# Row additions of the first expert round split between GpSimd and VectorE and tied behind the last gate product; a second convolution by transposes; a router shift summed before its product

## The chip, the cores and the metric

The kernel runs on one core of a Trainium2 chip. Its time is the device time in microseconds (us) of one execution; several runs are made and their median is taken. Lower is better. The engines are named as in the profile: PE (TensorE, matrix products and transposes), DVE (VectorE), ACT (ScalarE), POOL (GpSimd) and SP (SyncE, which here only issues transfers). Each engine works through its own instructions in order.

## The reference

Two layers of a diffusion backbone over 256 latent rows of width 1024, with 256 context rows that go through layer 0 whole and through layer 1 only as keys and values. What matters here is the end of a layer:

```python
    x = x + g1 * _merge(attn, hyena, gates, w_br_a, w_br_b, w_out)
    h2 = _rms(x, norm_ffn) * (1.0 + sc2) + sh2
    x = x + g2 * _hier_moe(h2.reshape(B * L, D), w_group, b_group, w_router, b_router,
                           moe_w1, moe_w3, moe_w2).reshape(B, L, D)
...
    for g in range(N_GROUPS):
        a = jnp.einsum('td,edf->tef', h, w1[g])
        b = jnp.einsum('td,edf->tef', h, w3[g])
        hid = jax.nn.silu(a) * b * cw[:, g, :, None]
        y = y + jnp.einsum('tef,efd->td', hid, w2[g], preferred_element_type=F32)
```

Of the 32 experts of a layer each row uses two. The context rows do the same with `g2c` in place of `g2`. Inside the merge, `hyena` is a long convolution of order two, `z = gate * (conv + z * skip)` once for each order.

## The kernel before

Rows are held in tiles of 128: in layer 0 four of them (`i` = 0 and 1 latent, 2 and 3 context), in layer 1 two. A framework places the instructions of each engine in an order that it fixes when the program is built.

**The first expert round** (`first_round`) takes the 32 experts in 16 pairs p; `q` counts 0 to 7 and each `q` holds the pairs 2q and 2q+1. For a pair, PE makes the product `w13` (tile `pW<-we,xT`, 32 recorded matmuls of 128x512), ACT the silu (`sl`), DVE the gate product `hd` (L1365), PE transposes it (`pX<-cst,hd`, L1368), ACT copies it (`hdT`), and PE makes `w2` (`pW<-we,hdT`, 16 recorded matmuls). I write hd(p), w13(p) and w2(p) for those of pair p. The weights come as loads of 1 MiB, six for a pair, from SP's queue into a ring of buffers; `fetch` issues a load when the buffer's last user has been put in the program.

The results of `q` < 6 are scattered by POOL to rows of a DRAM buffer `ybuf`. Those of `q` = 6 and 7 stay on the chip as `Y` and reach the rows by products with a selection matrix (`pG<-Y,PT`, `pQ<-Y,PT`, L1456). What was scattered is read back by `collect(i)`: two loads of 128x1024 from POOL's queue (`yr`, `yt`), and an inner function `add` with three VectorE operations of 128x1024: sum of the two, times the gate row `g2` (a broadcast, tile `bc`), added to `x`. `collect` of the first half of the tiles is called at `q` = 6, that of the rest at `q` = 7; the `add`s of each follow the next gate product in the code. After the pairs comes a branch for rows that found no place (`overflow`), which these inputs do not need.

**Layer 1's start** (`head`): the rows are normalised (`xn`, L457), transposed by PE, scaled, split in two parts (`hT`), and multiplied with the input weights in pieces; the first pieces give `u`, on which DVE does two operations a piece (L535, L537) for a short convolution before PE transposes it. The context rows' last additions (`rest`) stand in this stretch on DVE.

**The second convolution's output** is made in three places (layer 0 twice, layer 1 once) by 48 matmuls of 128x128 (`pB<-gt,Yh`), each followed on DVE by the product with `x2`. **The router's shift** (L890) is, in the same three cases, a product of a matrix of ones with eight slices of 128x36 (16 records).

## Time and profile before

| | before |
|---|---|
| median of 3 runs | 1447.03 us (1446.01 to 1447.13) |
| profiled execution, time | 1441.07 us |
| profiled execution, span | 1439.3 us |
| mean granted TensorE clock | 0.961 |
| PE busy | 1281.0 us, 89% |
| VectorE busy | 660.3 us, 46% |
| ScalarE busy | 455.8 us, 32% |
| GpSimd busy | 211.0 us, 15% |
| DMA, mean | 259 GB/s |

The profiled execution is one of its own, beside the three timed runs; the span goes from its first to its last instruction. PE is busy nearly everywhere, so the places to look at are the few where it stands still.

### The profile page before, as it was taken

To read this page: it belongs to the slowest core of one execution; us is meant where nothing else is said; L and a number is where in the kernel's file an instruction comes from. 1 tells how busy PE (TensorE), PEld (TensorE's weight loads), DVE (VectorE), ACT (ScalarE), POOL (GpSimd) and SP (SyncE) were. 2 spreads that over 40 slices of the span, in tenths; PEclk is the share of its full clock that TensorE was granted. 3 is DMA by queue.
4 is the path that set the end of the run, shared out by engine and by line. 5 is a ranking of instruction groups with operands and counts; after the bars stand their busy time and mean duration, and the time that the engine had idled before them with its cause. 6 is when DMAs were issued, how large, how long until landed. Compare 5 with 4: busy or idle time off the path is not lost. (4 is left out here: it accounts for less than half of the span.)

```text
span 1439.3 us, 18183 instructions
## 1 busy us (share of the span) xinstructions
PE 1281.0 (89%) x7071; PEld 831.1 (58%) x7071; DVE 660.3 (46%) x1361; ACT 455.8 (32%) x884; POOL 211.0 (15%) x175
## 2 busy tenths in 40 slices
PE   5999999999999999599888397999899969998776
PEld 2555777886578887344333134899779943443222
DVE  4654366676677666601000137865774760100014
ACT  3433223337632133222211014533574522221101
POOL 2021033361000000211110000032500021110000
PEclk9999999999999999699999699999999979999989
DMA  9744625455177762799999963325326749999991
GB/s 377 282 166 185 230 90 190 159 219 215 59 262 274 288 241 98 278 408 420 419 420 422 403 274 137 129 106 211 136 94 219 259 161 380 418 419 420 422 407 69
DMA packets 65691, 373.04 MB, mean 259 GB/s; under 512 B 11994, under 2 KB 13338, under 8 KB 26048
## 3 DMA queue, kind: packets, MB, share of 16 engines
q1 hardware_dynamic: 54368, 347.67, 61.9%
q0 software_dynamic: 10368, 21.02, 4.1%
q10 hardware_dynamic: 864, 3.15, 0.5%
q8 instruction: 57, 0.93, 0.3%
q14 instruction: 34, 0.28, 0.1%
HBM read 362.06 MB, written 27.53 MB: 271 GB/s over the span
## 5 line engine op out<-in xcount | busy, mean ns | idle before, releaser
L1411 PE MATMUL pW<-we,xT 128*64 128x512 f32 x1024 | 263.0, 605 | 8.5 <-DMA we<-in_wexp_dram 8.4
L1411 PEld LDWEIGHTS pW<-we,xT 128*64 128x64 f32 x1024 | 82.3, 138 | 149.8 <-issue 131.7
L239 PE MATMUL pA<-hT,wsp 128*128 128x512 f32 (+1 forms) x448 | 156.3, 349 | 4.0 <-ACT hf L223 4.0
L1365 DVE SCALAR_TENSOR_TENSOR hd<-sl,cws,pW 128x256 f32<-128x256 f32 x32 | 15.3, 480 | 305.9 <-ACT sl L223 305.9
L241 PE MATMUL pA<-hT,wsp 128*128 128x512 f32 (+1 forms) x448 | 154.4, 345 | 1.1 <-DVE wsp L220 1.1
L240 PE MATMUL pA<-hT,wsp 128*128 128x512 f32 (+1 forms) x448 | 154.0, 344 | 0.0
L220 DVE TENSOR_TENSOR wsp<-win,wsp 128x1024 fp32r<-128x1024 f32 x80 | 102.1, 1281 | 105.8 <-ACT wsp L223 105.6
L1426 PE MATMUL pW<-we,hdT 128*64 128x512 f32 x512 | 142.0, 621 | 4.9 <-ACT hdT L223 4.7
L223 ACT ACTIVATE wsp<-win 128x1024 fp32r<-128x1024 f32 x80 | 84.1, 1057 | 141.9 <-PE pA L241 137.2
L240 PE MATMUL pA<-wsp,hT 128*128 128x256 f32 x352 | 99.9, 284 | 2.6 <-DVE wsp L220 2.6
L239 PE MATMUL pA<-wsp,hT 128*128 128x256 f32 x352 | 100.2, 285 | 0.7 <-ACT vv L223 0.7
L241 PE MATMUL pA<-wsp,hT 128*128 128x256 f32 x352 | 99.7, 283 | 0.0
L239 PEld LDWEIGHTS pA<-hT,wsp 128*128 128x128 f32 x448 | 86.2, 192 | 21.6 <-issue 8.0
L240 PEld LDWEIGHTS pA<-hT,wsp 128*128 128x128 f32 x448 | 86.1, 192 | 13.7 <-issue 6.1
L241 PEld LDWEIGHTS pA<-hT,wsp 128*128 128x128 f32 x448 | 85.9, 192 | 11.1 <-issue 1.8
L1426 PEld LDWEIGHTS pW<-we,hdT 128*64 128x64 f32 x512 | 48.6, 141 | 73.3 <-issue 59.2
L223 ACT ACTIVATE Y<-pW 128x512 f32<-128x512 f32 (+1 forms) x64 | 38.2, 597 | 137.0 <-PE pW L1426 134.7
L223 ACT ACTIVATE sl<-pW 128x256 f32<-128x256 f32 x32 | 12.3, 383 | 218.7 <-PE pW L1411 218.7
L248 POOL TENSOR_TENSOR rs<-rsq,mh 128x1 f32<-128x1 f32 x14 | 8.4, 601 | 424.9 <-DVE rsq L247 414.0
L239 PEld LDWEIGHTS pA<-wsp,hT 128*128 128x128 f32 x352 | 67.3, 191 | 5.3 <-issue 2.5
L240 PEld LDWEIGHTS pA<-wsp,hT 128*128 128x128 f32 x352 | 67.4, 191 | 3.4 <-DVE wsp L220 3.2
L241 PEld LDWEIGHTS pA<-wsp,hT 128*128 128x128 f32 x352 | 67.4, 191 | 0.2
(301 smaller groups left out, 2324.4 us busy)
## 6 DMA issues: line engine op xcount, KB each, us to landing
we<-in_wexp_dram SPq DMA_DIRECT2D x190, 1024.0 KB
win<-in_win_dram SPq DMA_DIRECT2D x40, 1024.0 KB
ada<-in_ada_dram SPq DMA_DIRECT2D x32, 1024.0 KB
ada<-in_adaj_dram SPq DMA_DIRECT2D x16, 1024.0 KB
wbr<-in_wbr_dram SPq DMA_DIRECT2D x8, 1024.0 KB
wout<-in_wout_dram SPq DMA_DIRECT2D x8, 1024.0 KB
ybuf<-zero SPq DMA_DIRECT2D x12, 512.0 KB
bc<-modd SPq DMA_DIRECT2D x12, 512.0 KB
```

The source lines that it names most:

```text
L220: (eng or self.nc.vector).tensor_tensor(out=out, in0=a, in1=b, op=op)
L223: self.nc.scalar.activation(out, in_, func, **kw)
L239: self.nc.tensor.matmul(out, lh, rh, start=start, stop=False)
L240: self.nc.tensor.matmul(out, lh, rl, start=False, stop=False)
L241: self.nc.tensor.matmul(out, ll, rh, start=False, stop=stop)
L248: nc.gpsimd.tensor_tensor(out=out, in0=t, in1=self.mh[:, : shape[1]], op=ALU.pow)
L1365: nc.vector.scalar_tensor_tensor(out=hd, in0=sl, scalar=cws, in1=pa[:, 256:512], op0=ALU.mult, op1=ALU.mult)
L1411: nc.tensor.matmul(pa[64 * e : 64 * e + 64, :], xT[:, kc, cs], wt[(2 * p + e, kc // 4)][:, kc % 4, :], start=kc == 0, stop=kc == KC - 1)
L1426: nc.tensor.matmul(py[64 * e : 64 * e + 64, :], hdT[:, fc, 64 * e : 64 * e + 64], wt[(2 * p + e, 2)][:, fc, hs], start=fc == 0, stop=fc == 1)
```

## The change

Four things are done.

1. `collect` is called for the two latent tiles only, both at `q` = 6. The sum and the gate product move from DVE to POOL. Only `x += yr` and `x += yt` stay on DVE, and they are told to be placed behind the last `hd` then issued (`last_hd`, which is that of pair 15 when the order is made). In layer 1 one more buffer is needed for `yr`: it takes slot 15 of the weight ring, whose last turn goes without it.
2. In layer 0 the context tiles' rows are loaded at the end of the layer (tiles `yc`, and the gate row `gc`), summed and multiplied on POOL in layer 1's head, and added to `x` on DVE there.
3. The second convolution's output is made by 12 matmuls of 128x512 with the other operand held still, two ACT copies (`zr`) and 8 transposes.
4. The router's eight slices are summed by one VectorE reduction, so that one product is left.

```diff
@@ head of layer 1
             for i in tiles:
                 if not full and i > 1:
+                    self.tt(xs[1][:, i % 2, :], xs[1][:, i % 2, :], self.crows[i - 2][0], ALU.add)
                     for half in range(2):
                         self.residual(i, half, None)
...
             head([0, 1])
+            y0, y1, gc = self.crows[0]
+            first = nc.gpsimd.tensor_tensor(out=y0, in0=y0, in1=y1, op=ALU.add).ins
+            with self.tc.issue_after(first):
+                self.tt(y0, y0, gc, ALU.mult, nc.gpsimd)
+                y0, y1, gc = self.crows[1]
+                self.tt(y0, y0, y1, ALU.add, nc.gpsimd)
+                self.tt(y0, y0, gc, ALU.mult, nc.gpsimd)
@@ second convolution
+            zr = []
+            for r in range(2):
+                pz = self.ps("C")
+                for k2 in range(2):
+                    self.mm3(pz, (gt[:, 0, k2, r, :], gt[:, 1, k2, r, :]), (Yh[:, r, k2, :], Yl[:, r, k2, :]), k2 == 0, k2 == 1)
+                zr.append(self.T2([P, 512], name="zr"))
+                self.act(zr[r], pz)
             for cm in range(4):
                 pz = self.ps("B", [P, 2, P])
                 for r in range(2):
-                    for k2 in range(2):
-                        self.mm3(pz[:, r, :], (Yh[:, r, k2, cm * P : cm * P + P], Yl[:, r, k2, cm * P : cm * P + P]),
-                                 (gt[:, 0, k2, r, :], gt[:, 1, k2, r, :]), k2 == 0, k2 == 1)
+                    nc.tensor.transpose(pz[:, r, :], zr[r][:, cm * P : cm * P + P], self.ident)
@@ router
-            for kc in range(KC):
-                nc.tensor.matmul(pb, self.ones, wrs[:, s, kc, :], start=kc == 0, stop=kc == KC - 1)
+            V.tensor_reduce(out=bb[:, s], in_=wrs[:, s].rearrange("p k n -> p n k"), axis=AX.X, op=ALU.add)
+            nc.tensor.matmul(pb, self.ones, bb[:, s], start=True, stop=True)
@@ collect
-            if full and i % 2 == 0:
-                yr = self.S(21, [P, 2, D], name="yr")
+                yr = self.S(21 if full else 15, [P, 2, D], name="yr")
...
+            self.tt(yt[0], yt[0], yt[1], ALU.add, nc.gpsimd)
+            self.tt(yt[0], yt[0], g2[:, 0, :], ALU.mult, nc.gpsimd)
             def add():
-                x_ = xm[i // 2][:, i % 2, :]
-                self.tt(yt[0], yt[0], yt[1], ALU.add)
-                self.tt(yt[0], yt[0], g2[:, i // 2, :], ALU.mult)
-                self.tt(x_, x_, yt[0], ALU.add)
+                x_ = xm[0][:, i, :]
+                with self.tc.issue_after(self.last_hd):
+                    self.tt(x_, x_, yt[0], ALU.add)
             return add
@@ end of the layer, behind the overflow branch
+        if full:
+            gc = self.T4([P, D], name="gc")
+            nc.sync.dma_start(gc, self.modd[l, 3, 1:2, :].partition_broadcast(P)[:, 0, :])
+            self.crows = []
+            for i in (2, 3):
+                yr = self.S((17, 19)[i - 2], [P, 2, D], name="yc")
+                for k in range(2):
+                    nc.gpsimd.dma_start(yr[:, k, :], ybuf[(k * nt + i) * P : (k * nt + i) * P + P, :])
+                self.crows.append((yr[:, 0, :], yr[:, 1, :], gc))
@@ ring of layer 1
-            seq = [15, 18, 11, 13, 16, 21, 2, 3, 17, 19, 4, 5, 6, 7, 8, 9] * 6
+            seq = [15, 18, 11, 13, 16, 21, 2, 3, 17, 19, 4, 5, 6, 7, 8, 9] * 5
+            seq += seq[1:16] + [18]
@@ first_round
             if q == 7:
-                for u in adds:
-                    u()
-                adds = [collect(i) for i in range(nt // 2, nt)]
                 self.banks["X"] = [7]
...
             if q == 6:
-                adds = [collect(i) for i in range(nt // 2)]
+                adds = [collect(i) for i in range(2)]
```

**How the order moves.** On DVE, at the end of layer 0's first round, the order before is this (the rows `hd` are those of pairs 11 to 14 in turn, `x_4404` the latent rows):

```order
L1365 SCALAR_TENSOR_TENSOR hd_6036<-sl_6034,cws_5463,pW_5990 128x256
L220 TENSOR_TENSOR yr_6133<-yr_6133 128x1024
L220 TENSOR_TENSOR yt_6136<-yt_6136,yt_6137 128x1024
L1365 SCALAR_TENSOR_TENSOR hd_6122<-sl_6120,cws_5630,pW_6076 128x256
L220 TENSOR_TENSOR Y_6129<-pW_6143,Y_6129 128x512
L220 TENSOR_TENSOR Y_6129<-pW_6152,Y_6129 128x512
L1365 SCALAR_TENSOR_TENSOR hd_6185<-sl_6183,cws_5630,pW_6140 128x256
L220 TENSOR_TENSOR Y_6192<-pW_6229,Y_6192 128x512
L220 TENSOR_TENSOR Y_6192<-pW_6238,Y_6192 128x512
L1365 SCALAR_TENSOR_TENSOR hd_6259<-sl_6257,cws_5797,pW_6226 128x256
```

The order of the change there, from the gate product of pair 13 to behind that of pair 15:

```order
L1388 SCALAR_TENSOR_TENSOR hd_6133<-sl_6131,cws_5574,pW_6088 128x256
L220 TENSOR_TENSOR Y_6140<-pW_6177,Y_6140 128x512
L220 TENSOR_TENSOR Y_6140<-pW_6186,Y_6140 128x512
L1388 SCALAR_TENSOR_TENSOR hd_6207<-sl_6205,cws_5741,pW_6174 128x256
L220 TENSOR_TENSOR Y_6214<-pW_6218,Y_6214 128x512
L220 TENSOR_TENSOR Y_6214<-pW_6227,Y_6214 128x512
L1388 SCALAR_TENSOR_TENSOR hd_6268<-sl_6266,cws_5741,pW_6215 128x256
L220 TENSOR_TENSOR x_4348<-x_4348,yr_6077 128x1024
L220 TENSOR_TENSOR x_4348<-x_4348,yt_6082 128x1024
L220 TENSOR_TENSOR Y_6277<-pW_6288,Y_6277 128x512
```

The two row sums no longer stand ahead of hd(12); two additions to `x` stand behind hd(15) instead. Layer 1 shows the same with one row sum ahead of hd(12) before.

On POOL, between the reading back of the rows and layer 1's head, the order of the change is in two pieces, the first at the end of the round, the second behind the branch:

```order
L1318 DMA yr_6077<-ybuf_124 128x1024 x2
L1318 DMA yt_6082<-ybuf_124 128x1024
L1318 DMA yt_6083<-ybuf_124 128x1024
L220 TENSOR_TENSOR yr_6077<-yr_6077 128x1024
L220 TENSOR_TENSOR yt_6082<-yt_6082,yt_6083 128x1024
L220 TENSOR_TENSOR yr_6077<-yr_6077,bc_6074 128x1024
L220 TENSOR_TENSOR yt_6082<-yt_6082,bc_6074 128x1024
L1379 DMA yc_6576<-ybuf_124 128x1024 x2
...
L1379 DMA yc_6573<-ybuf_124 128x1024 x2
L993 DMA ft_7138<-in_fmain_dram 128x2048
L478 TENSOR_TENSOR yc_6573<-yc_6573 128x1024
L220 TENSOR_TENSOR yc_6576<-yc_6576 128x1024
L220 TENSOR_TENSOR yc_6573<-yc_6573,gc_6571 128x1024
```

Before, POOL had only the loads there. The loads of one context tile (`yc_6573`) now stand ahead of the load of `ft`, a table of the first convolution, and behind it come four POOL operations.

On DVE in layer 1's head, the change's order around the first pieces `u` is this (`x_4351` are the context rows):

```order
L543 SCALAR_TENSOR_TENSOR u_6672<-pA_6647,prm_6579,u_6672 128x255
L220 TENSOR_TENSOR x_4351<-x_4351,yc_6573 128x1024
L545 SCALAR_TENSOR_TENSOR u_6672<-pA_6647,prm_6579,u_6672 128x255
L220 TENSOR_TENSOR wsp_6747<-win_6280,wsp_6747 128x1024
L220 TENSOR_TENSOR vS_6643<-pA_6701,vS_6643 128x2x128
L543 SCALAR_TENSOR_TENSOR u_6706<-pA_6676,prm_6579,u_6706 128x255
L220 TENSOR_TENSOR x_4351<-x_4351,rest_6351 128x512
L545 SCALAR_TENSOR_TENSOR u_6706<-pA_6676,prm_6579,u_6706 128x255
```

Before, nothing of the context rows stood between the two operations of a piece: the additions of `rest` stood earlier, among the `hT` operations. Now the addition of POOL's product stands between the two operations of the first piece.

## Rows read from the trace of the kernel before

**Rows 1.** Stretches of layer 0's tail: us, busy us by engine, clock, DMA share, GB/s.

```profile
792.00:812.40 20.40, 0.00 (x0) 0.00 (x0) 2.33 (x2) 0.00 (x0) 1.70 (x4) 0.56 1.01 418
812.40:830.00 17.60, 16.44 (x56) 5.42 (x56) 1.90 (x4) 1.58 (x3) 0.54 (x1) 0.83 0.95 380
830.00:849.00 19.00, 16.91 (x61) 5.85 (x60) 2.03 (x4) 2.35 (x5) 0.00 (x0) 1.00 0.55 224
```

**Rows 2.** DVE's timeline, layer 0's tail: start, duration, instruction, idle before and releaser.

```profile
803.78 1.23 DVE L220 TENSOR_TENSOR yr<-yr 128x1024 f32<-128x1024 f32 x1 [28.20 <-DMA yr<-ybuf]
811.30 1.23 DVE L220 TENSOR_TENSOR yt<-yt,yt 128x1024 f32<-128x1024 f32 x1 [6.29 <-DMA yt<-ybuf]
812.44 0.48 DVE L1365 SCALAR_TENSOR_TENSOR hd<-sl,cws,pW 128x256 f32<-128x256 f32 x1
...
867.42 0.47 DVE L1365 SCALAR_TENSOR_TENSOR hd<-sl,cws,pW 128x256 f32<-128x256 f32 x1
```

**Rows 3.** PE's timeline, layer 0's tail.

```profile
812.97 0.69 PE L1368 MATMUL pX<-cst,hd 128*128 128x128 f32 x2 [22.84 <-DVE hd L1365]
814.14 5.72 PE L1426 MATMUL pW<-we,hdT 128*64 128x512 f32 x16 [0.47 <-ACT hdT L223]
...
849.37 0.44 PE L1368 MATMUL pX<-cst,hd 128*128 128x128 f32 x2 [0.99 <-DVE hd L1365]
850.28 3.71 PE L1426 MATMUL pW<-we,hdT 128*64 128x512 f32 x16 [0.47 <-ACT hdT L223]
...
867.95 0.44 PE L1368 MATMUL pX<-cst,hd 128*128 128x128 f32 x2 [3.39 <-DVE hd L1365]
868.86 5.37 PE L1426 MATMUL pW<-we,hdT 128*64 128x512 f32 x16 [0.47 <-ACT hdT L223]
```

**Rows 4.** POOL's timeline, layer 0's tail and layer 1's start.

```profile
791.49 1.16 POOL L1306 DMA_DIRECT2D yr<-ybuf  x2 [7.10 <-DMA ybuf<-Y,gi]
...
887.53 0.58 POOL L980 DMA_DIRECT2D ft<-in_fmain_dram  x1 [1.99 <-DMA yr<-ybuf]
```

**Rows 5.** Stretches of layer 1's tail, columns as in Rows 1.

```profile
1362.00:1376.00 14.00, 0.29 (x1) 0.00 (x0) 1.57 (x2) 0.38 (x1) 1.21 (x3) 0.59 1.02 421
1376.00:1393.00 17.00, 16.34 (x56) 6.25 (x56) 1.43 (x3) 1.96 (x4) 0.49 (x1) 0.84 1.01 415
1393.00:1409.00 16.00, 14.49 (x60) 5.67 (x60) 1.91 (x4) 1.96 (x4) 0.00 (x0) 1.00 0.74 295
1409.00:1424.00 15.00, 14.51 (x64) 6.13 (x66) 8.20 (x9) 2.35 (x5) 0.54 (x1) 1.00 0.12 44
```

**Rows 6.** Chain of waits that ended last, its first long piece.

```profile
1362.86 11.36 DMA yt<-ybuf
```

**Rows 7.** PE's timeline, layer 1's tail.

```profile
1376.11 0.69 PE L1368 MATMUL pX<-cst,hd 128*128 128x128 f32 x2 [13.81 <-DVE hd L1365]
...
1423.50 3.65 PE L1426 MATMUL pW<-we,hdT 128*64 128x512 f32 x16
```

**Rows 8.** GpSimd's groups, shapes apart: busy us, mean ns, idle before.

```profile
L220 POOL TENSOR_TENSOR Yj<-Yj,t 128x512 f32<-128x512 f32 x24 | 32.3, 1357 | 141.6 <-DVE t L220 121.4 <-ACT hf L223 20.2
L220 POOL TENSOR_TENSOR c<-qraw 128x512 f32<-128x512 f32 x2 | 4.0, 2000 | 0.0
```

**Rows 9.** DVE's timeline in layer 1's head: the second operation on the first piece `u`.

```profile
899.11 0.47 DVE L537 SCALAR_TENSOR_TENSOR u<-pA,prm,u 128x255 f32<-128x255 f32 x1
```

**Rows 10.** One second convolution: the stretch for tile `gt` alone (PE, PEld, POOL).

```profile
252.00:262.00 10.00, 5.69 (x48) 5.52 (x48) 0.00 (x0) 1.00 0.31 106
```

**Rows 11.** PE's timeline at full clock: two 128x512 matmuls, four transposes, one router's shift.

```profile
953.08 0.40 PE L239 MATMUL pC<-Yh,gt 128*128 128x512 f32 x1
953.31 0.40 PE L240 MATMUL pC<-Yl,gt 128*128 128x512 f32 x1
...
775.99 0.60 PE L1273 MATMUL pG<-cst,xg 128*128 128x128 f32 x4
...
519.52 1.87 PE L890 MATMUL pC<-rtr,cst 128*128 128x36 f32 x16
```

More of the change, by code (lines that the diff above doesn't have):

```diff
@@ L1364, in hidden @@
         hd = self.TH([P, 256], name="hd")
-        nc.vector.scalar_tensor_tensor(out=hd, in0=sl, scalar=cws, in1=pa[:, 256:512], op0=ALU.mult, op1=ALU.mult)
+        self.last_hd = nc.vector.scalar_tensor_tensor(out=hd, in0=sl, scalar=cws, in1=pa[:, 256:512],
+                                                      op0=ALU.mult, op1=ALU.mult).ins
         ptt = self.ps("X", [P, 2, P])
```

## The prediction, made before the change was run

> **What bounds the kernel now.** I read the page first: PE is busy 89% of the span, so what matters is where it stands still. I then followed the chain of waits from its end. Its first long piece is no work at all: DVE waits for rows read back from DRAM [rows 6]. Stretches around that place, and around the same place in layer 0, show PE at nothing for 20.4 us in one and 0.29 us busy of 14 in the other, while the transfers run at 418 and 421 GB/s [rows 1, 5]. The timelines give the reason. In layer 0 DVE waits 28.20 us for `yr`, then again for `yt`, and hd(12), which stands behind them in DVE's order, starts at 812.44, right when they are done [rows 2]. PE's next instruction has waited 22.84 us for that hd [rows 3]. In layer 1 the wait of PE is 13.81 us [rows 7]. Elsewhere in these rounds the transpose waits 0.99 us for its gate product [rows 3], which is the normal latency.
>
> Two things bound the tail, therefore: PE's own work from hd(12) on, and the weight stream, which was not stopped by the stall. A removed stall is worth only what the stream allows.
>
> **The change, part by part.**
>
> *Layer 0's tail.* The row sums leave DVE; hd(12) is then set by its silu. The wait shrinks from 22.84 to 0.99: 21.85 us. After the stall the granted clock is 0.56, then 0.83 on average, where it was 1.00 [rows 1]: between the two levels of 2.4 and 1.2 GHz. So w2(12) took 5.72 us where w2(14) took 3.71 [rows 3]: 2.01 more. Behind hd(14), the additions of the context tiles delayed hd(15): PE waited 3.39 instead of 0.99 (2.40), and w2(15) took 5.37 instead of 3.71 (1.66). Sum: 27.9 us. Now the stream. From 792 to 849 it moved 20.4 x 418 + 17.6 x 380 + 19 x 224 kB = 19.5 MB [rows 1]; at 418 GB/s without a pause that is 46.6 us, so the last weights land at about 838.6. PE would come to w2(15) at 868.86 - 21.85 - 2.01 - 2.40 = 842.6. The cushion of 4 us is smaller for earlier pairs, since six loads of 1 MiB take 15.1 us at this rate, a little less than PE's pair; I take off 1 us. **Term: -27.** Bounds: -28, and -22 where the stream runs at the 380 GB/s of the middle stretch (19.5 MB then take 51 us, the last weights land at 843 and the pairs come about 5 us later).
>
> The two additions to `x` behind hd(15) cost 2 x 1.23 us on DVE [rows 2]. They are covered by the transposes, the copy and half of w2(15) (0.44, 0.47, 1.86), which must end before DVE's next `Y`; uncovered they would cost 2.5. They need POOL's products: two sums and two gate products of 128x1024. No such operation stands in the trace; POOL's 128x512 take 1.357 to 2.000 us [rows 8], so twice that, 2.7 to 4.0, and I take 3.2. Four of them are 13 us after the rows have landed near 804, thus by some 820, before hd(15) at about 841. The gate row `bc` keeps its place in SP's order.
>
> *Layer 1's tail.* 13.81 - 0.99 = 12.8 us. The clock after it is 0.84 over 17 us [rows 5], which by layer 0's measure is worth 2.0 to 2.7: I take 2.4. Sum 15.2; w2(15) would start at 1423.50 - 15.2 = 1408.3. The stream moved 14 x 421 + 17 x 415 + 16 x 295 + 15 x 44 kB = 18.3 MB from 1362 on, 43.5 us at 421 GB/s: the last weights land at 1405.5, again a little ahead of PE. The ring is one buffer shorter in its last turn, 15 MiB instead of 16, two and a half pairs deep: no wait from that. What follows w2(15) (to 1439.3) is the same work. **Term: -15**, bounds -16 and -10.
>
> *Layer 1's head.* This part costs. The context rows are no longer finished in layer 0's tail. POOL issues the loads of the last context tile about where it issued `ft` before, 887.53 in that trace's time [rows 4]. Landing: 1 MB at 418 GB/s is 2.5 us at the least; under the full stream it was 803.78 - 791.49 = 12.3 us [rows 2, 4]. The stream is over here, so I stay near the low end: 5.5. Then POOL does sum, sum, gate product before DVE can add the first: three of 3.2 us (2.7 to 4.0). Ready at 902.6; bounds 898 and 912. In DVE's order this addition now stands between the two operations of the first piece `u`, of which the second ran at 899.11 [rows 9]. It would run at 902.6 + 1.2 = 903.8: 4.7 us late, and PE, whose next transposes need `u`, waits about as long, with perhaps 1.3 us of lower clock behind it, as the pauses above had. Behind the stuck addition on DVE are `wsp` and `vS`, also PE's inputs, so nothing hides it. The four `rest` additions leave the stretch of the first `hT`, which returns a little. **Term: +6**, bounds 0 and +16 (912 + 1.2 - 899.1 = 14, and 2 for the clock).
>
> *Second convolution, three times.* 48 matmuls take 5.69 us [rows 10]. The new form has 12 matmuls at 0.23 (953.31 - 953.08) and 8 transposes at 0.15 (0.60 / 4) [rows 11]: 2.8 + 1.2 = 4.0. Saved 1.7, less what PE waits for the two copies by ACT, which share one bank: I take 0.6. **Term: 3 x -1.1 = -3.3**, bounds 0 and -5.
>
> *Router, three times.* 16 records in 1.87 us [rows 11] become two, 0.23. Saved 1.6, less a possible wait for DVE's new reduction; I take 1.4. **Term: 3 x -1.4 = -4.2**, bounds 0 and -4.9.
>
> **Sum.** -27 - 15 + 6 - 3.3 - 4.2 = -43.5 us. The profiled execution took 1441.07, so 1397.6; the median of the three runs stands 6.0 above it, and I put the same difference on the median: 1447.03 - 43.5 = **1403.5 us**.
>
> **Rivals.**
>
> *The stream holds the tails.* For it: it runs at 1.01 of its share through both stalls, and fell to 380 GB/s when PE came back [rows 1, 5]. Against it: both last landings come out 3 to 4 us before PE needs them. If so, layer 0 gives 22 and layer 1 gives 10: 1403.5 + 10 = 1413.5.
>
> *The head's stall is the large one.* POOL's four operations and DVE's `hT`, `wsp` and additions to `x` run in the same stretch. For it: POOL's 128x512 vary from 1.357 to 2.000 us on average [rows 8], as if something held them up at times. If each of POOL's operations holds a DVE operation up for its own 3.2 us and is itself held up for 1.2, the product comes 3.6 us later and DVE loses up to 3 x 3.2 = 9.6: +13 on the head, 1416.5. Against it: DVE waits there anyway, idle, in the main case. The Trainium skill, SBUF — State Buffer, section "Who interferes with whom", has such a rule: VectorE's `tensor_tensor` with both inputs in SBUF and GpSimd's reads share one port pair that is held for a whole instruction. By that rule the head would come out as in this rival; the spread of POOL's means agrees with it but has other possible reasons.
>
> *POOL's products hold up the last pair: slower than before.* `x += yr` stands in DVE's order behind hd(15) and ahead of `Y`, on which the rest of the tail hangs in both layers. If POOL's operation of 128x1024 took T, the four come 4T after the rows (near 804 in layer 0, 1374 at the latest in layer 1) and must be done by 841 and 1407: free up to T = 8. Beyond that each layer's tail loses 4T - 35 and the head 3T - 10. With T = 16 that is 29 + 29 + 38 = 96, and the time is far above before; the sign turns where 2 x (4T - 35) + 3T - 10 - 6 = 43.5, that is T = 11.8. Against it: no POOL operation on half the size averages above 2.0 us [rows 8]. The time at T = 13 would be 1403.5 + 34 + 23 = 1460.
>
> *The stall only moves.* The additions still end up ahead of a gate product. The order rules this out for DVE; there remains that the gate row or the rows land so late that hd(15)'s followers wait, giving the tails back. Then what is left is convolution and router, less the head: 1447.03 - 7.5 + 6 = 1445.5, no measurable change.
>
> **How the numbers follow.** Main case 0.66 (its own range 1394 to 1411), stream 0.12, larger head 0.15, no change 0.03, slower 0.04. Both middle rivals are still far below before, so faster by over 0.2% (2.9 us, about what a measurement can tell from no change) has 0.93, within it 0.03, slower 0.04. The range for 8 in 10: below, the bounds at their best are -28 - 16 + 0 - 5 - 4.9 = -54, 1393, and I go to 1391; above, both middle rivals together are 1403.5 + 10 + 13 = 1426.5, and I stop at 1423.
>
> **What would show it.** In layer 0's tail and layer 1's, PE's stretches without work are gone, the transposes of pair 12 wait about 1 us, and DVE's two additions stand behind hd(15) without delaying `Y`. In layer 1's head DVE's addition of the first context tile waits for POOL some 5 us and PE with it. The second convolution's 12 matmuls and 8 transposes take about 4 us, the router's shift a quarter of one. It is wrong if PE waits for weights in pairs 13 to 15 longer than 1 or 2 us (stream), if the head stands still over 10 us, or if POOL's operation takes longer than 4.

## The result and the profile after the change

The changed kernel takes 1411.76 us (median of 4 runs, 1409.93 to 1413.15), the one before 1446.52 us beside it (4 runs, 1443.29 to 1447.13): a ratio of 0.9763, 95% interval 0.9743 to 0.9784. The forecast was 1403.5 us in a range of 1391 to 1423. The gain is 34.8 us where 43.5 was forecast. PE is busy 90% of a shorter span, against 89% before. Each step went the predicted way; two terms of the sum did not have their size. One later execution of the changed kernel, at 6936.88 us, is left out of every figure below.

The page of the profiled execution after (1409.93 us), its span and its first part:

```profile
span 1408.1 us, 17963 instructions
PE 1274.3 (90%) x6945; PEld 822.6 (58%) x6945; DVE 646.8 (46%) x1352; ACT 458.4 (33%) x890; POOL 239.9 (17%) x187
```

To see where the 31.2 us between the two profiled spans went, I read the start of the same PE instruction in both timelines. The last column is the sum of all that lies ahead, so a term is the step from one line to the next:

| PE instruction | before, us | after, us | shift |
|---|---|---|---|
| router's shift, layer 0 (`rtr,cst`) | 519.5 | 517.0 | -2.5 |
| gate transposes of pair 11, layer 0 | 775.8 | 769.5 | -6.3 |
| end of w2(15), layer 0 | 874.2 | 843.2 | -31.0 |
| first projection of layer 1 | 893.3 | 861.1 | -32.2 |
| first second-convolution product, layer 1 | 953.1 | 935.1 | -18.0 |
| last `pC<-rtr,pq` products, layer 1 | 1254.4 | 1232.6 | -21.9 |
| w13(12), layer 1 | 1355.2 | 1333.1 | -22.1 |
| end of the span | 1439.3 | 1408.1 | -31.2 |

So layer 0's tail gives 24.7 of the forecast 27 and 1.2 more on the way into layer 1; layer 1's head costs 14.2 where 6 was forecast; layer 1's tail gives 9.1 of 15. The steps that are left, in which the convolutions and routers lie, give 10.4 where 7.5 was forecast for these.

PE's timeline of layer 0's tail after the change (start us, duration us, instruction, in brackets the idle time before it and what ended it), which answers to [rows 3]:

```profile
785.39 0.44 PE L1392 MATMUL pX<-cst,hd 128*128 128x128 f32 x2 [0.99 <-DVE hd L1388]
786.30 3.71 PE L1451 MATMUL pW<-we,hdT 128*64 128x512 f32 x16 [0.47 <-ACT hdT L223]
...
799.80 3.65 PE L1436 MATMUL pW<-we,xT 128*64 128x512 f32 x14 [2.68 <-DMA we<-in_wexp_dram]
...
838.57 0.44 PE L1392 MATMUL pX<-cst,hd 128*128 128x128 f32 x2 [0.99 <-DVE hd L1388]
839.48 3.70 PE L1451 MATMUL pW<-we,hdT 128*64 128x512 f32 x16 [0.47 <-ACT hdT L223]
```

The wait of 22.84 us is 0.99, w2(12) runs in 3.71 us in place of 5.72, and pair 15's transposes no longer wait 3.39. One wait is new: 2.68 us for pair 13's weights. DVE's timeline of the same place after the change, to be held against [rows 2]:

```profile
784.85 0.48 DVE L1388 SCALAR_TENSOR_TENSOR hd<-sl,cws,pW 128x256 f32<-128x256 f32 x1 [15.60 <-ACT sl L223]
...
838.43 1.22 DVE L220 TENSOR_TENSOR x<-x,yr 128x1024 f32<-128x1024 f32 x1
839.57 1.22 DVE L220 TENSOR_TENSOR x<-x,yt 128x1024 f32<-128x1024 f32 x1
...
842.95 0.69 DVE L220 TENSOR_TENSOR Y<-pW,Y 128x512 fp32r<-128x512 f32 x1 [2.17 <-ACT Y L223]
```

hd(12) now waits for its silu alone, and the two additions fill idle time behind hd(15): the next `Y` still waits 2.17 us for ACT. Their cover held. GpSimd's products for them were ready only at 827.5, since the gate row `bc` came late (GpSimd waited 15.67 us for it, up to 822.80); that is 7.5 us after the forecast's 820 and still 11 us before the additions.

GpSimd's timeline after the change, layer 0's tail and then layer 1's head:

```profile
797.26 2.33 POOL L220 TENSOR_TENSOR yr<-yr 128x1024 f32<-128x1024 f32 x1 [9.83 <-DMA yr<-ybuf]
...
856.29 1.17 POOL L1379 DMA_DIRECT2D yc<-ybuf  x2 [1.88 <-DVE xn L458]
...
865.92 2.39 POOL L478 TENSOR_TENSOR yc<-yc 128x1024 f32<-128x1024 f32 x1 [7.92 <-DMA yc<-ybuf]
868.26 2.38 POOL L220 TENSOR_TENSOR yc<-yc 128x1024 f32<-128x1024 f32 x1
870.60 4.63 POOL L220 TENSOR_TENSOR yc<-yc,gc 128x1024 f32<-128x1024 f32 x2
```

The operation that no trace of before showed takes 2.33 to 2.39 us, below the lower bound of 2.7. What came late is the rows: issued at 856.29, used at 865.92, so 9.6 us and not 5.5. They were not alone. SyncE issued `gc` (512 KB, at 855.80), `H` (1024 KB) and `rt` (162 KB, at 856.72) within the same microsecond, and `ft` (1024 KB) followed on GpSimd's queue. SyncE's issue of `H`, GpSimd's of `ft`, and the stretches of this flight (columns: us, busy us and count of PE, PEld, DVE, ACT, POOL, granted clock, DMA share, GB/s):

```profile
856.24 0.38 SPq L606 DMA_DIRECT2D H<-Hd  x1
857.45 0.54 POOL L993 DMA_DIRECT2D ft<-in_fmain_dram  x1
```

```profile
856.30:861.00 4.70, 3.65 (x16) 2.12 (x16) 4.03 (x11) 2.42 (x6) 1.70 (x3) 0.57 0.68 264
861.00:865.90 4.90, 4.78 (x22) 4.78 (x23) 2.47 (x8) 1.44 (x4) 0.00 (x0) 0.50 1.03 416
```

With these rows that is 3.8 MB, for which 416 GB/s would need about 9.2 us (an estimate from the sizes and this rate). No run takes the other loads away. DVE's and then PE's timeline of the same head, after the change:

```profile
867.25 0.48 DVE L543 SCALAR_TENSOR_TENSOR u<-pA,prm,u 128x255 f32<-128x255 f32 x1 [3.61 <-ACT u L223]
872.97 3.35 DVE L220 TENSOR_TENSOR x<-x,yc 128x1024 f32<-128x1024 f32 x1 [5.24 <-POOL yc L220]
876.24 0.47 DVE L545 SCALAR_TENSOR_TENSOR u<-pA,prm,u 128x255 f32<-128x255 f32 x1
...
886.85 1.21 DVE L220 TENSOR_TENSOR x<-x,yc 128x1024 f32<-128x1024 f32 x1
```

```profile
876.86 0.68 PE L521 MATMUL pA<-cst,u 128*128 128x128 f32 x2 [7.04 <-DVE u L545]
```

DVE stands idle for 5.24 us and then spends 3.35 us on an addition that takes 1.21 alone. It began when the first product ended, while GpSimd's second ran to 875.2 (870.60 + 4.63); it ended 1.1 us after that. PE's next transposes wait 7.04 us for the piece behind it.

Layer 1's tail in PE's timeline after the change, for [rows 7]:

```profile
1341.15 0.44 PE L1392 MATMUL pX<-cst,hd 128*128 128x128 f32 x2 [0.99 <-DVE hd L1388]
...
1351.40 8.78 PE L1436 MATMUL pW<-we,xT 128*64 128x512 f32 x30 [3.16 <-DMA we<-in_wexp_dram]
...
1383.69 0.61 PE L1451 MATMUL pW<-we,hdT 128*64 128x512 f32 x1 [0.54 <-DMA we<-in_wexp_dram]
...
1392.75 3.65 PE L1451 MATMUL pW<-we,hdT 128*64 128x512 f32 x16
```

Here too the stall on the gate product is gone, all 12.8 us of it, and a wait for pair 13's weights has come, with w13(13) at 8.78 us instead of 7.08 behind it. A part of the wait had only changed its place. The stretches of that tail after the change (columns as above) show the stream at 419 to 420 GB/s up to 1375:

```profile
1330.00:1355.00 25.00, 18.98 (x76) 7.16 (x75) 1.86 (x3) 3.54 (x7) 5.53 (x6) 0.94 1.02 420
1355.00:1375.00 20.00, 18.54 (x80) 7.02 (x77) 1.86 (x3) 1.96 (x4) 3.58 (x2) 0.99 1.01 419
```

### The profile page after: what moved, and what is told of

Its sections match the earlier page's. It is cut to its first block, busy times and chain, and to the rows that moved or that the text cites. A ratio compares the mean times of both kernels' runs of the same rounds, so it can differ in the third digit from the quotient of the medians.

```text
span 1408.1 us, 17963 instructions
## 1 busy us (share of the span) xinstructions
PE 1274.3 (90%) x6945; PEld 822.6 (58%) x6945; DVE 646.8 (46%) x1352; ACT 458.4 (33%) x890; POOL 239.9 (17%) x187
## 5 line engine op out<-in xcount | busy, mean ns | idle before, releaser
L239 PE MATMUL pA<-hT,wsp 128*128 128x512 f32 (+1 forms) x448 | 158.4, 354 | 1.1 <-ACT hf L223 1.1
L241 PE MATMUL pA<-hT,wsp 128*128 128x512 f32 (+1 forms) x448 | 156.5, 349 | 1.1 <-DVE wsp L220 1.1
L240 PE MATMUL pA<-hT,wsp 128*128 128x512 f32 (+1 forms) x448 | 156.1, 348 | 0.0
L1451 PE MATMUL pW<-we,hdT 128*64 128x512 f32 x512 | 136.4, 598 | 5.4 <-ACT hdT L223 4.7
L239 PEld LDWEIGHTS pA<-hT,wsp 128*128 128x128 f32 x448 | 88.2, 197 | 18.8 <-issue 8.0
L240 PEld LDWEIGHTS pA<-hT,wsp 128*128 128x128 f32 x448 | 88.0, 196 | 14.0 <-issue 6.1
L241 PEld LDWEIGHTS pA<-hT,wsp 128*128 128x128 f32 x448 | 87.7, 196 | 11.2 <-issue 1.8
L223 ACT ACTIVATE sl<-pW 128x256 f32<-128x256 f32 x32 | 12.3, 383 | 226.0 <-PE pW L1436 226.0
```

Of the source, the lines that this page charges most:

```text
L223: self.nc.scalar.activation(out, in_, func, **kw)
L239: self.nc.tensor.matmul(out, lh, rh, start=start, stop=False)
L240: self.nc.tensor.matmul(out, lh, rl, start=False, stop=False)
L241: self.nc.tensor.matmul(out, ll, rh, start=False, stop=stop)
L1451: nc.tensor.matmul(py[64 * e : 64 * e + 64, :], hdT[:, fc, 64 * e : 64 * e + 64], wt[(2 * p + e, 2)][:, fc, hs], start=fc == 0, stop=fc == 1)
```

## Experiments

Twelve kernels ran, one of them the change itself. Medians are compared with the change (1411.76) unless said otherwise; every one also had the kernel before beside it, at 1444 to 1447 us.

**Convolution and router alone.** The kernel before, with only the changes to the second convolution and to the router's shift.

```diff
+ zr.append(self.T2([P, 512], name="zr"))
+ self.act(zr[r], pz)
...
+ nc.tensor.transpose(pz[:, r, :], zr[r][:, cm * P : cm * P + P], self.ident)
...
+ V.tensor_reduce(out=bb[:, s], in_=wrs[:, s].rearrange("p k n -> p n k"), axis=AX.X, op=ALU.add)
+ nc.tensor.matmul(pb, self.ones, bb[:, s], start=True, stop=True)
```

> The kernel before with the second convolution and the router's shift of the change alone; the first expert round and layer 1's head are as before. My theory: these two parts are PE work taken away where PE is the bound, each three times, so the whole gives what the two traces show at marks on PE: 2.1 + 1.5 us for the convolutions and 3.1 + 1.5 us for the router, together 8.2 us, about 1438.5 us against 1446.5. Rival: PE's shortened stretches only run into the next weight load, and the expert rounds, whose weight stream keeps them busy, swallow most of it; then 2 us or less are left, 1444.5 or more.

1435.69 us (1433.56 to 1439.54), ratio to before 0.9942 (0.9919 to 0.9965): 9.6 us less by the medians, 8.4 by the ratio. The interval is 5.1 to 11.7 us, so the sum of the two terms (7.5) stands and the rival that these parts are hidden (2 us or less) falls; the run does not separate the two. The rest of the change is therefore worth 25 to 26 us net.

**The context rows' addition tied later.** In the change, DVE's `x += yc` came between the two operations of the first piece `u`. Here it is tied behind the second operation of the fourth piece.

```diff
+ stt = nc.vector.scalar_tensor_tensor(out=uv[:, :, 0:255], ...)
+ if m == 3:
+     self.last_u = stt.ins
...
- self.tt(xs[1][:, i % 2, :], xs[1][:, i % 2, :], self.crows[i - 2][0], ALU.add)
+ with self.tc.issue_after(self.last_u):
+     self.tt(xs[1][:, i % 2, :], xs[1][:, i % 2, :], self.crows[i - 2][0], ALU.add)
```

> The changed kernel with one edit: in layer 1's head the two additions of the context products to x are placed on DVE behind the second operation of the fourth piece u, instead of between the two of the first. The products themselves stay on POOL. My theory: the 7.0 us that PE waits for the first piece come from this place alone, and the products are ready when the fourth piece is done; PE's wait goes, the lower clock before it stays, and the second half of the loss (the context rows are late for their transposes) shrinks a little: 7 to 9 us less than the changed kernel, about 1404 us. Rival: what costs is DVE's crowding in this stretch, 9.9 of 10 us busy, and POOL and DVE holding each other up; then the place is of no account, and at most 2 us come back, 1410 or more.

1405.22 us (1402.57 to 1406.55), ratio to before 0.972 (0.9704 to 0.9737): 6.5 us faster than the change, just short of the theory's 7 to 9 and well above the rival's 2; it is the fastest kernel here that computes everything. PE's wait of 7.04 us for the first piece is gone. From layer 1's first projection to the first product of its second convolution it takes 66.9 us; before it was 59.8, in the change 74.0. Half the loss remains, 4.07 us of it as a wait of PE for the context rows. DVE's timeline of that head, this kernel, and GpSimd's beneath it:

```profile
870.44 2.42 DVE L220 TENSOR_TENSOR wsp<-win,wsp 128x1024 fp32r<-128x1024 f32 x1
```

```profile
869.37 2.41 POOL L479 TENSOR_TENSOR yc<-yc 128x1024 f32<-128x1024 f32 x1 [7.97 <-DMA yc<-ybuf]
871.73 3.39 POOL L220 TENSOR_TENSOR yc<-yc 128x1024 f32<-128x1024 f32 x1
```

The two engines take turns. `wsp`, 1.21 us in the change, is issued at 870.44 and ends at 872.86, which is 1.1 us after GpSimd's first sum ended (871.78); GpSimd's second sum, issued at 871.73, ends 2.3 us after that `wsp`. Each holds the other up for a whole instruction. The Trainium skill, SBUF — State Buffer, section "Who interferes with whom", says so of VectorE's `tensor_tensor` with both inputs in SBUF and of a GpSimd instruction that reads SBUF: one shared port pair, held exclusively. These rows agree with it. The operations on `u` and `vS`, which read PSUM, keep their 0.4 to 0.5 us meanwhile.

**The latent rows back on DVE, tied.** Sums and gate products of the tail run on DVE again, but all behind the last hd.

```diff
- self.tt(yt[0], yt[0], yt[1], ALU.add, nc.gpsimd)
- self.tt(yt[0], yt[0], g2[:, 0, :], ALU.mult, nc.gpsimd)
...
  with self.tc.issue_after(self.last_hd):
+     self.tt(yt[0], yt[0], yt[1], ALU.add)
+     self.tt(yt[0], yt[0], g2[:, 0, :], ALU.mult)
```

> The changed kernel with the latent rows' sums and gate products back on DVE, all six operations tied behind the last gate product; POOL only loads these rows. The context rows are as in the change. My theory: the stall ahead of pair 12 was the place in DVE's order, not the engine, so both tails keep their gain; but four more operations of 1.14 us stand ahead of Y in each tail, where DVE has 2.2 us (layer 0) and 1.6 us (layer 1) to spare, so each tail loses about 2.5 to 3 us: 5 to 6 us more than the changed kernel, about 1417 us. Rival: moving the sums to POOL is what removed the stall; then the time goes back by the two stalls, 20 us or more, 1432 or more.

1420.33 us (1417.01 to 1421.98): 8.6 us slower than the change, somewhat above the expected 5 to 6, and far from the rival's 1432. PE's timeline of layer 0's tail, this kernel:

```profile
847.30 0.50 PE L1480 MATMUL pG<-Y,PT 128*128 128x512 f32 x1 [1.38 <-DVE Y L220]
...
850.16 0.50 PE L1480 MATMUL pG<-Y,PT 128*128 128x512 f32 x1 [2.14 <-DVE Y L220]
```

Six operations of 1.22 us stand ahead of `Y`, and PE waits for it. The place behind hd(15) is free for two operations, not for six.

**The tie taken out.** GpSimd keeps sums and products; the framework chooses where `x += yr` stands.

```diff
- with self.tc.issue_after(self.last_hd):
-     self.tt(x_, x_, yt[0], ALU.add)
+ self.tt(x_, x_, yt[0], ALU.add)
```

> The changed kernel without the tie: sums and products stay on POOL, the framework places the two additions to x itself, which it does behind the gate product of pair 14 instead of pair 15, in both layers. My theory: POOL's products were ready at 827.5 in layer 0 and 1378.4 in layer 1 of the changed kernel's profile, the gate products of pair 14 ran at 822.3 and 1376.6; so DVE waits 5 us and 2 us there, holding up Y of pair 14 but not the next gate product, which comes 14 us later: within 2 us of the changed kernel, 1410 to 1414. Rival: without the tie the stall comes back, one layer or both, 10 us or more, 1422 or more.

1412.9 us (1411.31 to 1413.59), 1.1 us above the change with overlapping runs: no difference that these runs can tell. Untied, DVE's timeline has the additions ahead of hd(15), 3 us after GpSimd's products were ready (830.5):

```profile
833.64 1.22 DVE L220 TENSOR_TENSOR x<-x,yr 128x1024 f32<-128x1024 f32 x1
834.77 1.22 DVE L220 TENSOR_TENSOR x<-x,yt 128x1024 f32<-128x1024 f32 x1
842.05 0.48 DVE L1387 SCALAR_TENSOR_TENSOR hd<-sl,cws,pW 128x256 f32<-128x256 f32 x1 [6.06 <-ACT sl L223]
```

With this and the run before: either half of the edit alone, the move to GpSimd or the tie, removes the stall; in both kernels and both layers the transposes of pair 12 wait 0.99 us. The move leaves DVE two operations in place of six; once it is made, the tie adds nothing that can be measured.

**Small reads in layer 1.** To test whether the read-back is what delays pair 13's weights. The kernel leaves out most of these rows' sums.

```diff
+ w = D if full else 64
+ if not full:
+     nc.gpsimd.memset(yt[k], 0.0)
- nc.gpsimd.dma_start(yt[k], ybuf[...])
+ nc.gpsimd.dma_start(yt[k][:, 0:w], ybuf[..., 0:w])
```

> The changed kernel, but in layer 1 the four reads of the scattered rows fetch 64 columns of 1024 (the rest of the buffers is set to zero on POOL), so most of those rows' sums is left out; all else stays. My theory: the reads, 2.1 MB, stand in the transfers ahead of pair 13's weights, which come 5 us later for it; that is why the changed kernel's PE waits 3.16 us there and runs that product at the lower clock (8.78 instead of 7.08). Without them the wait and the slow product go: 4 to 5.5 us less than the changed kernel, about 1407 us. Rival: the wait comes from the weight ring, which is one buffer shorter in its last turn; then the reads are of no account, and it is within 1 us, 1411 or more.

1409.15 us (1404.78 to 1409.67), ratio to before 0.974 (0.9718 to 0.9763): 2.6 us faster by the median, less than the theory's 4 to 5.5 and more than the rival's 1, with intervals that overlap. The trace is clearer than the median. PE's timeline of layer 1's tail, this kernel:

```profile
1353.74 7.08 PE L1439 MATMUL pW<-we,xT 128*64 128x512 f32 x30 [1.49 <-DMA we<-in_wexp_dram]
```

The wait is 1.49 in place of 3.16 and w13(13) takes its 7.08 (granted clock 1.00, against 0.81 in the change). From pair 12's transposes to pair 15's (1345.42 to 1391.02) it is 45.6 us, against 50.6 in the change and 46.4 before; the nine other edited kernels that read these rows whole take 49.85 to 50.98 there. The read-back costs these 5 us; in this execution's span (1407.4) an earlier part hides most of it: pair 12's transposes come 4.3 us later than in the change, 4.1 of them already at layer 1's first projection (865.21), ahead of the edited place. The ring is as short as in the change, so it is not the cause of these 5 us; the 1.49 that is left is not explained.

**The first read later.** So let the read of `yr` come later, into a buffer that comes free later.

```diff
- yr = self.S(21 if full else 15, [P, 2, D], name="yr")
+ yr = self.S(21 if full else 9, [P, 2, D], name="yr")
...
- seq += seq[1:16] + [18]
+ seq += seq[0:15] + [15]
```

> The changed kernel with another buffer for layer 1's yr: slot 9, whose last user is a product of pair 13, in place of slot 15, free two and a half pairs earlier; the ring's last turn is as long as in the change. The two reads of yr go out some 20 us later, behind the weights of pair 13. My theory: half of the 2.1 MB leaves the place ahead of those weights, 2.5 us of transfer, PE's wait of 3.16 us there shrinks by about that, and the products are still ready before they are wanted: 2 to 3.5 us less than the changed kernel, about 1409. Rival: the stream as a whole is what ends late, bytes are bytes wherever they stand, and pair 14 or 15 waits instead: within 1 us of the changed kernel.

1413.58 us (1411.73 to 1414.62), ratio to before 0.9779 (0.9759 to 0.9799): no gain. The theory fell. GpSimd's and PE's timelines of layer 1's tail, this kernel:

```profile
1342.47 1.17 POOL L1318 DMA_DIRECT2D yt<-ybuf  x2 [7.58 <-DMA ybuf<-Y,gi]
1354.47 2.34 POOL L220 TENSOR_TENSOR yt<-yt,yt 128x1024 f32<-128x1024 f32 x1 [10.83 <-DMA yt<-ybuf]
1362.36 1.11 POOL L1318 DMA_DIRECT2D yr<-ybuf  x2 [5.55 <-DMA we<-in_wexp_dram]
```

```profile
1354.12 8.78 PE L1436 MATMUL pW<-we,xT 128*64 128x512 f32 x30 [3.50 <-DMA we<-in_wexp_dram]
```

`yr` did go 22 us later, and w13(13) waits as long as ever (3.50). The other tile's rows now go first, and their 1 MB is on its way from 1342.47 to 1354.47, the time in which pair 13's weights should come. In the change both tiles were issued at once, and the first one landed 12.3 us later (1340.39 to 1352.65), the second after w13(13) had begun. If the queue serves them in turn, only the first megabyte was ever in the way, and moving the second helps nobody. That reading fits both traces; no run isolates it.

**Context rows read before the branch.** `yc` of the first context tile gets a buffer that is free earlier, GpSimd's sums stand behind `rs`, and the addition is tied behind the second piece.

```diff
- yr = self.S((17, 19)[i - 2], [P, 2, D], name="yc")
+ yr = self.S((12, 19)[i - 2], [P, 2, D], name="yc")
...
+ with self.tc.issue_after(self.rs_tie):
      first = nc.gpsimd.tensor_tensor(out=y0, in0=y0, in1=y1, op=ALU.add).ins
```

> The changed kernel with the context rows' part mended in three ways: the last context tile is read into slot 12, which the overflow branch does not use, so its reads stand ahead of the branch; POOL's sums stand behind the two rs operations; DVE's additions to x are tied behind the second piece u. My theory: of the 14 us that layer 1's head loses in the change, 7 are the first piece's wait, gone already with the tie behind the fourth piece (1405.2 us), and the other 7 come from the context rows being late for their transposes; with products ready some 8 us earlier, 3 to 5 of these come back: about 1401 us. Rival: the rest is POOL and DVE holding each other up, which only moves to the hT operations of the first piece: 1405 or more.

1412.46 us (1411.32 to 1413.52), 7.2 us slower than the version tied behind the fourth piece: the theory (about 1401) fell, and the rival (1405 or more) held. The rows came earlier, and with them the collisions. DVE's timeline, and PE's first projection, this kernel:

```profile
862.52 3.38 DVE L220 TENSOR_TENSOR wsp<-win,wsp 128x1024 fp32r<-128x1024 f32 x1
...
866.33 2.89 DVE L220 TENSOR_TENSOR hT<-hf,hT 128x256 fp32r<-128x256 f32 x2
869.14 2.63 DVE L230 CAST hT<-hf 128x256 fp32r<-128x256 f32 x2
```

```profile
873.17 0.58 PE L239 MATMUL pA<-hT,wsp 128*128 128x256 f32 x1 [7.13 <-ACT hf L223]
```

Two `hT` differences take 2.89 us in place of 0.75, two casts 2.63 in place of 0.49, and the first projection waits 7.13 us for `hT` where it waited 1.15.

**Both of these.** The late read of `yr` put on top of the version just shown.

```diff
- yr = self.S((17, 19)[i - 2], [P, 2, D], name="yc")
+ yr = self.S((12, 19)[i - 2], [P, 2, D], name="yc")
...
- seq += seq[1:16] + [18]
+ seq += seq[0:15] + [15]
```

> The mended context part and layer 1's later reads of yr together. My theory: the two places are 400 us apart and have nothing to do with each other, so the gains add: 2 to 3.5 us less than the kernel with the mended context part alone, about 1398 us. Rival: the later reads gain nothing by themselves, then it is the same as that kernel within 1 us.

1411.16 us (1407.82 to 1412.32), 1.3 below the one before it with overlapping runs: inconclusive. In the trace w13(13) waits 3.49 us, so nothing for the late read.

**Context rows on DVE.** To remove the collisions, the context tiles' sums and products go back to DVE, behind the fourth piece.

```diff
- first = nc.gpsimd.tensor_tensor(out=y0, in0=y0, in1=y1, op=ALU.add).ins
...
  with self.tc.issue_after(self.last_u):
+     self.tt(y0, y0, y1, ALU.add)
+     self.tt(y0, y0, gc, ALU.mult)
      self.tt(xs[1][:, i % 2, :], xs[1][:, i % 2, :], y0, ALU.add)
```

> The changed kernel with the context rows' sums and products on DVE as well, all six operations placed behind the second operation of the fourth piece u; POOL only loads these rows. Compared with the kernel in which only the two additions are placed there (1405.2 us) and the sums and products run on POOL. My theory: while POOL's four operations run, DVE's operations with both inputs on the chip are held up (wsp 2.3 to 2.4 us instead of 1.22); with POOL idle DVE gets some 3.5 us back there and pays 4.6 for the four operations: within 2 us of that kernel, 1403 to 1407. Rival: POOL's help is real and DVE, busy 9.6 to 9.9 of 10 us here, pays each added operation in full with what it delays: 4 us or more on top, 1409 or more.

1411.49 us (1405.74 to 1413.02), 6.3 us slower than with GpSimd at the same tie; the theory (within 2 us) fell. DVE's and PE's timelines of the head, this kernel:

```profile
872.94 1.23 DVE L220 TENSOR_TENSOR wsp<-win,wsp 128x1024 fp32r<-128x1024 f32 x1
```

```profile
895.95 1.12 PE L466 MATMUL pA<-cst,xn 128*128 128x128 f32 x4 [6.22 <-DVE xn L462]
900.43 1.11 PE L466 MATMUL pA<-cst,xn 128*128 128x128 f32 x4 [3.37 <-DVE xn L462]
```

The collisions are gone (`wsp` is 1.23 again), but four more operations on DVE make the normalized context rows `xn` late, and PE waits 9.6 us for them. DVE has no room in this stretch.

**Tied later still.** The context addition behind the sixth piece instead of the fourth.

```diff
- if m == 3:
+ if m == 5:
      self.last_u = stt.ins
```

> The changed kernel with the two additions of the context products placed behind the sixth piece u instead of the fourth (1405.2 us there). My theory: what is left of the head's loss is the context rows coming late to their transposes, for which PE waited 4.07 us with the tie behind the fourth piece; two pieces later they come about 6 us later, less what PE finds to do meanwhile: 3 to 6 us more, 1408 to 1411. Rival: that wait is set by POOL's operations and by rs, not by the additions' place; then it is the same within 1.5 us.

1416.7 us (1413.63 to 1419.58), 11.5 us slower than behind the fourth; the direction was expected, not the size. PE's timeline has 6.82 us of waiting for DVE in one place, the first convolution's products:

```profile
895.66 0.80 PE L239 MATMUL pB<-vS,ft 128*128 128x512 f32 x1 [6.82 <-DVE Yj L220]
```

The framework moved other DVE work as well, so this run does not price the tie by itself.

**The change once more**, unedited, beside the last two.

> The changed kernel itself once more, beside the last experiments, to see what one kernel's median moves from one chip visit to the next: 1411.8 us within 2 us.

1410.28 us (five executions, 1408.57 to 1414.65). Differences of 1 to 2 us between the medians of these runs mean nothing; those of 6 and more do.

**Without the context rows' work.** The change, less GpSimd's four operations and DVE's two additions in layer 1's head.

```diff
- self.tt(xs[1][:, i % 2, :], xs[1][:, i % 2, :], self.crows[i - 2][0], ALU.add)
...
- first = nc.gpsimd.tensor_tensor(out=y0, in0=y0, in1=y1, op=ALU.add).ins
...
```

> The changed kernel without the work on the second half of the context rows in layer 1's head: GpSimd's sums and products and VectorE's two additions are left out (the loads stay), so layer 1 goes on with wrong rows there. Theory (the head's loss is this work: late rows, operations of GpSimd and VectorE that hold each other up, and the context rows that come late for their transposes): from layer 1's first projection to its first second-convolution product it takes 60 to 62 us in place of 74, PE waits for no first piece u, and the median is 1397 to 1400 us, 12 to 15 below the change. Rival (half of the head's loss has another cause, a lower clock after the tail or the additions of rest that moved): that stretch takes 65 us or more and the median is 1403 us or more.

1400.26 us (1399.31 to 1401.35), ratio to before 0.969 (0.9672 to 0.9707): 11.5 us below the change, a hair outside the band of 1397 to 1400 that the theory gave, and below the rival's 1403. DVE's timeline of the head, this kernel:

```profile
861.19 0.68 DVE L220 TENSOR_TENSOR x<-x,rest 128x512 f32<-128x512 f32 x1
...
870.99 0.48 DVE L537 SCALAR_TENSOR_TENSOR u<-pA,prm,u 128x255 f32<-128x255 f32 x1
871.38 1.22 DVE L220 TENSOR_TENSOR wsp<-win,wsp 128x1024 fp32r<-128x1024 f32 x1
```

The two operations on the first piece follow each other, and from the first projection (865.35) to the first product of the second convolution (924.96) it takes 59.6 us, as before the change (59.8). The whole loss of the head comes with this work. But the run takes away more than the six operations: the `rest` additions, which add to the same rows, stand at 861.19 to 865.70 again, among the first `hT` operations as before, where in the change they followed `x += yc` from 878.72 on. So it shows what the work costs together with the order that it forces on DVE, and does not rule out the rival's `rest` additions as a part of that.

## Why the prediction was right, and where it was off

*How close it was.* The median came out 8.3 us above the forecast. By the profiled executions, from which the terms were read, the miss is 12.3 us (1397.6 forecast, 1409.93 measured): before's stood 5.5 us below its median, the change's only 1.8. Losses of 2.3, 5.9 and 8.2 us in the tails and the head are partly made up by 4.1 us more in the remaining steps. At 1411.76 us the result lies just above the main case's own range (1394 to 1411); the whole range holds it because it was drawn around two rivals, and parts of both came true. The mechanism of the gain was right; that the number came this close is in part luck.

*What bound the kernel* was read rightly. A DVE order that put rows from DRAM ahead of gate products stopped PE in both layers; both stalls are gone but for the usual 0.99 us, and either half of the edit would have done it. (The granted clock of 0.56 is that of the stall's own stretch and not of the time after it, which has 0.83 [rows 1]; the term itself was taken from the times of w2 and holds.)

*Layer 0's tail* (-27, measured -24.7). The stall was worth 21.3 us by the starts (812.97 to 785.39, less 6.3 that came from ahead), the clock's share in w2(12) 2.01 and pair 15 as counted. The difference is the new wait of 2.68 us for pair 13's weights. My cushion of 4 us was figured for the last landing, and 1 us was taken off for the earlier pairs; pair 13 had the least. That the rows read back just ahead of it are the reason is shown for layer 1 below, not for layer 0.

*The cover of the additions and GpSimd's duration.* Cover as predicted. The duration is 2.35 us, not 3.2: not even the lower bound held, as twice the 128x512 rows of [rows 8] overstates it. The slower-than-before rival needed 11.8 and was never near.

*Layer 1's tail* (-15, bounds -16 and -10, measured -9.1): the first step that failed. The 12.8 us of the stall came off whole, and of the 2.4 us that I put on the clock 2.3 were gained between pair 12's transposes and w13(13); but w13(13) now waits 3.16 us and runs 1.70 longer than 7.08, and pair 14 takes 1.7 longer up to w2(15), with a wait of 0.54 in it. I checked that the last weights land in time (they do), and not pair 13's, when 2.1 MB of rows go the same way at 420 GB/s. The run with small reads shows that these reads are the cause: the tail's stretch is 5.0 us shorter. The rival in which the stream holds the tails was thus half true in layer 0 (24.7, between its 22 and my 27) and true in size in layer 1 (9.1 against its 10). My own sign for it, waits of more than 1 or 2 us for weights in pairs 13 to 15, came in both layers (2.68 and 3.16).

*Layer 1's head* (+6, bounds 0 and +16, measured +14.2): the second, and the larger one. Up to PE's first transposes of `u` the loss is 8.4 us. Of what I had worked out there, the landing was 9.6 us and not 5.5 (+4.1), three GpSimd operations 7.1 and not 9.6 (-2.5), the addition 3.35 and not 1.2 (+2.1). The landing rested on "the stream is over here": the weight stream was, the transfers were not, as 264 and then 416 GB/s during the flight show. The longer addition is the rival's mechanism, at a smaller size: that rival asked for up to 9.6 us on DVE. Behind the transposes come 5.8 us more that I had covered only with 1.3 us for the clock: the context rows reach `xn` late, 30.0 and 35.8 us behind the first projection (891.11 and 896.91) where it was 3.3 and 7.4 before, in a stretch in which DVE has no reserve, as this window of the change shows (columns as above):

```profile
886.00:926.00 40.00, 35.89 (x258) 33.12 (x257) 38.94 (x76) 22.35 (x40) 11.49 (x8) 0.96 0.46 162
```

DVE is busy 38.94 of 40 us. I named the work behind the stuck addition and priced the wait only; that the rows' later users are then late too was left out, and the `rest` additions, whose move I counted as a small gain, now stand behind the stuck addition and ahead of `xn`. The run without this work shows all of it, 14.4 us in the trace, 11.5 in the median. How the 7 us that remain with the tie behind the fourth piece split between taking turns and late rows is open: the runs that removed one of the two made the other larger.

*Convolution and router* (-7.5, measured 8.4 alone) came out as counted, within that run's interval. PE's timeline after the change, second convolution and layer 0's router:

```profile
257.71 0.39 PE L241 MATMUL pC<-Yh,gt 128*128 128x512 f32 x1
257.94 0.40 PE L239 MATMUL pC<-Yh,gt 128*128 128x512 f32 x1
...
258.64 0.38 PE L670 MATMUL pB<-cst,zr 128*128 128x128 f32 x2
...
517.03 0.30 PE L903 MATMUL pC<-rtr,cst 128*128 128x36 f32 x2
```

The products follow each other at 0.23 us, a pair of transposes takes 0.38, and the shift is 0.30 where 16 records took 1.87 [rows 11].

## What to carry to other kernels

Work moved to an idle engine is priced by the place at which its result is waited for: find the receiving engine's instruction behind it, and that instruction's readers, before calling it hidden. Where a removed stall lets compute catch up with a saturated stream, check each buffer's landing and not only the last, with every other transfer that comes earlier too. Before a landing is taken to be short, list the loads that are issued in the same microseconds. GpSimd's operations and VectorE's with both inputs in SBUF took turns here: count a whole instruction of the one on each long operation of the other.

## What the hardware showed that I had not expected

GpSimd's 128x1024 sum takes 2.33 to 2.39 us alone and up to 3.4 beside DVE; DVE's 1.22 us operation grows to 2.3 to 3.38 beside it, and a pair of 128x256 casts from 0.49 to 2.63. On GpSimd's queue a read of 1 MB took 12.0 to 12.3 us from issue to first use while SyncE's weight stream ran at 418 to 420 GB/s, where 1 MB at that rate is 2.5 us; it took 12.0 also where no second read was issued beside it (the run with the late `yr`). In layer 1's head it took 9.6 us, beside four other loads and at up to 416 GB/s in all.
